# Padding small matmuls, cutting the prompt's value products to 32-column tiles with the sample's runs behind them, and pacing the sample's work over two stages

## The chip, the cores and the metric

The kernel runs on one core of one Trainium2 chip. The metric is the device time of one execution in microseconds (us). Before the change it is 3110.48 us, the median of three runs from 3101.09 to 3113.35.

The core's engines each run a list of instructions of their own, in the order that was laid out for it: TensorE (PE in the profile, with its weight loads as PEld), VectorE (DVE), ScalarE (ACT), GpSimd (POOL) and SyncE (SP). SP issues nearly all DMAs here.

## The reference, cut to what matters

One inference step of a decoder: one recurrent layer (RG-LRU), then one attention layer with forget gates that reads keys and values made once from the residual stream. It is done for a prompt of 2048 new tokens and for a sample of 8 sequences with 8 new tokens each, whose 4096 past tokens lie in pages of a cache.

```python
def fox_block(q, k, v, cq, ck, q_pos, k_pos):
    s = jnp.einsum('bqhd,bkhd->bhqk', q, k).astype(jnp.float32) * (HEAD_DIM ** -0.5)
    s = s + jnp.swapaxes(cq, 1, 2)[:, :, :, None] - jnp.swapaxes(ck, 1, 2)[:, :, None, :]
    mask = k_pos[None, :] <= q_pos[:, None]
    s = jnp.where(mask[None, None], s, -jnp.inf)
    p = jax.nn.softmax(s, axis=-1)
    return jnp.einsum('bhqk,bkhd->bqhd', p.astype(v.dtype), v)
```

There are 16 heads of 64 values. All data is float32. The keys and values of the past are 8 x 4096 rows of 16 x 64, read through `page_table`.

## The kernel before, in words

The program is written in an order that a builder then lays out on the engines: it keeps dependencies, and places ready instructions by priority (their place in the program) on a simulated time line. `tc.high_priority()` raises the priority, `tc.issue_after(i)` keeps instructions of an engine behind `i` on it. What the engines see is one fixed order each.

**Stages.** The recurrent layer over the prompt's halves, with the projections of the first half, comes first. The sample's decoding is cut into 16 turns (a sequence and half of the heads, `turns` at L1709); two are done early. Then `shared` (L1678) projects the prompt's second half to keys, values, queries and gates (`phase_b`), six steps alone and from about 1260 to 1703 us with the sample's work beside it; from 1703 to 2905 us `attention` (L1301) runs the prompt's attention, and `project` (L1589) makes the output rows until the end. The other 14 turns are the side work of the two middle stages.

**Side work.** `Side.along` (L1010) lets the main generator take a step, adds the cost that it yields, and takes as many steps of the side generator as bring its own cost to `share` times that (L1780). The side generator `beside` (L1774) is `decode` (L1024) and then `project_ready` (L1575), which loads and splits the output weights. The costs are written by hand: a turn yields `TURN` (L1019), 22,615.

**A turn of `decode`.** `keys` loads a quarter of a MB a page, four pages at a time (`pages`, L1053, on SP's queue into one of four `raw` buffers), transposes them on DVE (L1149), and after four such loads `scores` (L1113) does 64 matmuls of 128 x 32 with 128 moving columns in four column tiles. `new_scores` (L1127) does 32 small ones on 32 rows for the sample's own keys. `softmax` (L1157) finds the maxima (two small transposes, L1170 and L1175), exponentials and sums, and sends the probabilities through DRAM to another layout. `values` (L1217) loads the value pages and does 16 matmuls of 128 x 32 with 256 moving columns per four pages (`products`, L1225), at the end those of the new rows (L1235) and the sums over column tiles (L1257). One matmul of full float32 operands appears in the profile as two. `period` (L1265) interleaves the values of one turn with the keys of the next. A turn loads 64 pages: 32 of keys and 32 of values, for 8 of the 16 heads.

**The prompt's attention.** A unit (L1346) is a head and a block of 512 queries; the order of blocks turns round from head to head. For each of up to 16 blocks of 128 keys, two matmuls make the scores (`st`, L1527 and L1528, two PSUM buffers), on the diagonal a third adds the mask (L1530), ACT takes the exponential (L1536), and POOL sums the probabilities into `acc` (L1553; five buffers). After every fourth key block `product` (L1538), two steps later, multiplies the four blocks' probabilities by the values: the even blocks to one half of the PSUM tile's rows, the odd ones to the other, so that two tiles of 64 columns run side by side (L1547). `together` (L108) keeps such a group of matmuls in one piece. In between, `top` (L1384) computes the scores of later units in another layout for their maxima (`sx`, L1394, reduced on DVE), and `tops` (L1403) turns the maxima into rows by a transpose of 4 columns (L1411). `finish` (L1419) moves a unit's result out of PSUM; `total` (L1445) sums the four `acc` of a head by matmuls of 32 columns (L1450); `norm` (L1461) spreads the reciprocals by a matmul on 16 rows, or 4 in the last head (L1474), and multiplies by the gate. `later` (L339) is a list of calls by due step.

## Time and profile before

| | |
|---|---|
| median of three runs | 3110.48 us (3101.09 to 3113.35) |
| the profiled execution | 3106.18 us, its span 3104.4 us |
| TensorE's mean granted clock over the span | 0.958 |
| HBM read, written | 513.82 MB, 135.16 MB |
| sample's last value product ends | about 2580 us of the span |
| the prompt's last unit ends | about 2905 us |

A profile page gives busy time by engine, the chain of work that ended last (followed back from the end to what released each step) and the costliest groups of instructions. A group's line names the source line, engine, operation, the tile written and those read, the tile of the array in rows*columns, the moving operand and its count; then busy us, mean ns of one, and idle time of the engine just before with what ended it. A time line gives start and length in us, and the instructions merged in a row (`x16`). The ends of matmuls are modelled, so the starts are what to read there.

### The profile page before, as it was taken

Reading aid. Unit: us, or ns where it says so; the run is one execution under the profiler, and the core shown is the slowest. Engines: PE = TensorE matmul, PEld = TensorE weight load, DVE = VectorE, ACT = ScalarE, POOL = GpSimd, SP = SyncE. Lnnn points to the kernel's source line nnn. Section 1 sums busy time; section 2 is a strip of 40 time slices with the busy share of each in tenths; the row PEclk is TensorE's granted clock in tenths of the full one; section 3 lists DMA queues with packets and bytes.
Section 4 is the critical chain, followed back from the end, with each engine's and each line's share of the span. In section 5 each row is a group of like instructions: output and inputs, shape, how many; then the busy total and the mean of one; then the engine's idle time right before and its main releaser. Section 6 shows DMA issues by size and latency. Waiting matters only on the chain.

```text
span 3104.4 us, 58085 instructions
## 1 busy us (share of the span) xinstructions
PE 2856.4 (92%) x20446; PEld 2185.3 (70%) x20446; DVE 1805.1 (58%) x4014; ACT 1293.3 (42%) x2874; POOL 1155.4 (37%) x1251
## 2 busy tenths in 40 slices
PE   6998998998999989998998889898899989999798
PEld 5997888988999978886886555554555544544587
DVE  7876555424367756755755766666677655543244
ACT  4665432232346655333332344343444445455221
POOL 1653201000026531000002456565565757688322
PEclk9999999999999999998999899898999999999899
DMA  3225447788622266999999989999999985331343
GB/s 120 90 76 151 150 136 213 242 269 255 199 78 87 87 189 215 327 319 314 329 337 294 287 271 285 303 279 297 283 325 304 312 254 181 91 86 40 96 131 113
DMA packets 492854, 653.23 MB, mean 210 GB/s; under 512 B 91100, under 2 KB 292829, under 8 KB 485286
## 3 DMA queue, kind: packets, MB, share of 16 engines
q1 hardware_dynamic: 488934, 643.87, 66.2%
q10 hardware_dynamic: 3340, 3.56, 0.4%
q8 instruction: 161, 2.64, 0.3%
q0 software_dynamic: 288, 2.10, 0.2%
q14 instruction: 131, 1.07, 0.1%
HBM read 513.82 MB, written 135.16 MB: 209 GB/s over the span
## 4 chain that ended last, share of the span: by engine, by line
PE 45%; DMA 20%; DVE 7%; SPq 5%; ACT 4%; issue 3%; POOL 1%; ACTq 0%; DVEq 0%; POOLq 0%
PE ops L1547 6%; DMA raw<-in_cache_k_dram 4%; PE st L1527 4%; DMA raw<-in_cache_v_dram 4%; PE sx L1394 3%; PE y L368 3%; PE y L369 3%; PE y L370 3%; PE st L1528 3%; PE dO L1229 3%; PE dS L1119 3%; SPq L1066 2%; PE kv L368 2%; PE kv L369 2%; PE kv L370 2%
## 5 line engine op out<-in xcount | busy, mean ns | idle before, releaser
L106 POOL TENSOR_TENSOR acc<-acc,p 128x512 f32<-128x512 f32 (+3 forms) x576 | 638.6, 1109 | 315.9 <-PE ops L1547 263.8
L1536 ACT ACTIVATE p<-st 128x512 f32<-128x512 f32 (+3 forms) x576 | 288.5, 525 | 399.1 <-PE st L1528 203.0
L1149 DVE STREAM_TRANSPOSE ktr<-raw 128x1024 f32<-128x1024 f32 x256 | 305.6, 1223 | 147.9 <-DMA raw<-in_cache_k_dram 133.4
L1396 DVE TENSOR_REDUCE mxs<-sx 128x1 f32<-128x512 f32 x384 | 254.5, 681 | 165.7 <-PE sx L1394 164.5
L368 PE MATMUL kv<-wh,xh 128*128 128x256 f32 (+3 forms) x1088 | 311.8, 291 | 6.4 <-ACT wh L412 6.2
L369 PE MATMUL kv<-wl,xh 128*128 128x256 f32 (+3 forms) x1088 | 308.9, 287 | 4.4 <-DVE wl L413 4.2
L370 PE MATMUL kv<-wh,xl 128*128 128x256 f32 (+3 forms) x1088 | 309.4, 287 | 0.0
L1547 PE MATMUL ops<-p,vvt 128*64 128x512 f32 (+3 forms) x1152 | 294.6, 552 | 3.2 <-ACT p L1536 3.1
L1527 PE MATMUL st<-qa,ka 128*128 128x512 f32 (+3 forms) x640 | 277.1, 433 | 19.4 <-ACT p L1536 17.0
L1394 PE MATMUL sx<-kbt,qbt 96*128 96x512 f32 (+3 forms) x640 | 238.4, 433 | 31.2 <-DMA qbt<-qd 13.9
L1527 PEld LDWEIGHTS st<-qa,ka 128*128 128x128 f32 x640 | 125.7, 196 | 175.1 <-issue 114.5
L1528 PE MATMUL st<-qbt,kbt 128*128 128x512 f32 (+3 forms) x640 | 241.1, 378 | 0.0
L412 ACT ACTIVATE wh<-wst,gv 128x256 fp32r<-128x256 f32 (+1 forms) x384 | 164.3, 499 | 174.1 <-DMA wst<-in_b_w_in_dram 66.2
L413 DVE SCALAR_TENSOR_TENSOR wl<-wst,gv,wh 128x256 fp32r<-128x256 f32 (+1 forms) x384 | 170.6, 494 | 111.1 <-ACT wh L412 106.9
L368 PE MATMUL qg<-xh,wh 128*128 128x384 f32 (+2 forms) x640 | 228.2, 357 | 1.0 <-ACT wh L412 1.0
L370 PE MATMUL qg<-xh,wl 128*128 128x384 f32 (+2 forms) x640 | 226.9, 355 | 2.3 <-DVE wl L413 2.3
L369 PE MATMUL qg<-xl,wh 128*128 128x512 f32 (+2 forms) x640 | 227.3, 357 | 0.0
L1084 POOL TENSOR_TENSOR qw<-qb,amask 128x128 f32<-128x128 f32 x64 | 28.7, 455 | 504.6 <-PE dS L1119 358.6
L368 PEld LDWEIGHTS kv<-wh,xh 128*128 128x128 f32 (+1 forms) x1088 | 204.1, 189 | 14.5 <-ACT wh L412 7.1
L369 PEld LDWEIGHTS kv<-wl,xh 128*128 128x128 f32 (+1 forms) x1088 | 204.0, 189 | 7.7 <-DVE wl L413 5.7
L370 PEld LDWEIGHTS kv<-wh,xl 128*128 128x128 f32 (+1 forms) x1088 | 205.2, 189 | 2.9 <-issue 2.5
L1394 PEld LDWEIGHTS sx<-kbt,qbt 96*128 96x128 f32 x640 | 120.0, 204 | 102.9 <-issue 36.4
(283 smaller groups left out, 6482.2 us busy)
## 6 DMA issues: line engine op xcount, KB each, us to landing
raw<-in_cache_k_dram SPq DMA_DIRECT2D x512, 256.0 KB
raw<-in_cache_v_dram SPq DMA_DIRECT2D x512, 256.0 KB
wst<-in_w_kv_dram SPq DMA_DIRECT2D x48, 512.0 KB
wst<-in_b_w_in_dram SPq DMA_DIRECT2D x48, 512.0 KB
xt<-in_x_prompt_dram SPq DMA_DIRECT2D x32, 512.0 KB
wst<-in_a_w_in_dram SPq DMA_DIRECT2D x64, 256.0 KB
x<-x SPq DMA_DIRECT2D x32, 512.0 KB
out_dram<-kf SPq DMA_DIRECT2D x128, 128.0 KB
```

What stands on the lines that cost most here:

```text
L106: eng.tensor_tensor(out, a, b, op=op)
L368: T.matmul(ps, lh(k), rh(k), start=(k == 0), stop=False)
L369: T.matmul(ps, lh(k), rl(k), start=False, stop=False)
L370: T.matmul(ps, ll(k), rh(k), start=False, stop=(k == nk - 1))
L413: V.scalar_tensor_tensor(wl[:, k, :], st[:, k, :], gk, f(wh[:, k, :]), op0=ALU.mult, op1=ALU.subtract)
L1149: V.transpose(t.kts[pp][:, n], raw[:, :, pp * 256:(pp + 1) * 256])
L1394: T.matmul(ps[:, :w], qb[0:96, j * P:(j + 1) * P], kb[0:96, ck * 512:ck * 512 + w], start=True, stop=True)
L1396: V.reduce_max(mx[:, j, ck:ck + 1], ps[:, :w], axis=AX.X)
L1527: T.matmul(ps[:, lo:], ka[:, ks], qa[:, lo:], start=True, stop=False)
L1528: T.matmul(ps[:, lo:], kb[:, ks], qb[:, lo:], start=False, stop=(k < qc * 4))
L1536: pair.append((k, lo, p, A.activation(p[:, lo:], ps[:, lo:], AF.Exp)))
L1547: return T.matmul(ops[r:r + HD, lo:], vvs[h % 2][:, k, :], p[:, lo:], start=(k < 2), stop=(last and k >= todo[-1][0] - 1))
```

## The change

Five things are changed. The matmuls on few rows or columns (maxima of the sample, new keys and values, the prompt's row maxima, the gate's reciprocals) get operands of all 128 rows, and the transposed ones of 128 columns, with zeros around the data in tiles that are zeroed once. The prompt's value products are cut into column tiles of 32, four side by side. While attention runs, the sample's score and value runs and the heads' totals are no longer put in place at their point of the program but kept in a list (`Aside`), and those that were listed before the present step are emitted after each value product with their first matmul held behind that product's last one and at high priority; a need of their result empties the list earlier. The sums over a turn's column tiles become one of these calls. The share becomes the side work's whole cost (with 16,000 for `project_ready`) over 0.96 of the two stages' costs, 331,563 and 615,942 by the formula, in place of 1.13 times the turns' cost over 331,563 + 950,000.

```diff
-SHARE = 1.13
+EVEN = 0.96
...
+    behind = [None]
...
-        first = mms[0]().ins
+        with ExitStack() as es:
+            if behind[0]:
+                es.enter_context(tc.high_priority())
+                es.enter_context(tc.issue_after(behind[0]))
+            first = mms[0]().ins
...
             tc.add_manual_dep(first, d.ins.name, SYNC)
+        ins = first
...
             for mm in mms[1:]:
-                mm()
+                ins = mm().ins
+        return ins
+    class Aside:
+        def __init__(self):
+            self.live, self.q = False, []
+        def __call__(self, fn, key=None):
+            if self.live:
+                self.q.append((later.t, key, fn))
+            else:
+                fn()
+        def flush(self, ins=None, t=None):
+            while self.q and (t is None or self.q[0][0] < t):
+                behind[0] = ins
+                got = self.q.pop(0)[2]()
+                ins = ins and got
+            behind[0] = None
+        def waits(self, key):
+            return any(k == key for _, k, _ in self.q)
+        def need(self, key):
+            if self.waits(key):
+                self.flush()
+    aside = Aside()
...
-        rawn = pool.tile([32, 512], F32, name="rawn")
+        rawn = pool.tile([P, 512], F32, name="rawn")
         G.memset(rawn[:, :], 0.0)
+        pcs = [pool.tile([P, 64], F32, name=f"dpc{i}") for i in range(2)]
+        for pc in pcs:
+            G.memset(pc[:, :], 0.0)
+        mx = pool.tile([P, P], F32, name="dmx")
+        G.memset(mx[:, :], 0.0)
+        mr = pool.tile([P, 16, DS], F32, name="dmr")
+        G.memset(mr[:, :, :], 0.0)
...
-                together([partial(score, h, x, a) for h in range(4) for x in range(2) for a in range(4)])
+                ins = together([partial(score, h, x, a) for h in range(4) for x in range(2) for a in range(4)])
...
+                return ins
...
             def new_scores(raw):
-                kx = (spare() if ahead else pool.tile([P, 512], F32, name="kx", tag="kx"))[:32, :512]
+                kx = (spare() if ahead else pool.tile([P, 512], F32, name="kx", tag="kx"))[:, :512]
...
                 sp = bank("dS")
-                for h in range(8):
-                    for x in range(2):
-                        blk = (h * 2 + x) * 32
-                        T.matmul(sp[:32, h * DS:(h + 1) * DS], qw[:32, h // 2, h % 2 * 2 + x, :], kx[:, blk:blk + DS],
-                                 start=(x == 0), stop=(x == 1))
+                def score(h, x):
+                    blk = (h * 2 + x) * 32
+                    return T.matmul(sp[:32, h * DS:(h + 1) * DS], qw[:, h // 2, h % 2 * 2 + x, :], kx[:, blk:blk + DS],
+                                    start=(x == 0), stop=(x == 1))
+                ins = together([partial(score, h, x) for h in range(8) for x in range(2)])
...
+                return ins
...
                     fetch_c()
+                    aside.need("values")
...
                     if n == 3:
-                        dl.after(1 + pp, lambda g=g, pp=pp, kt=t.kts[pp]: scores(g, pp, kt))
+                        dl.after(1 + pp, lambda g=g, pp=pp, kt=t.kts[pp]: aside(lambda: scores(g, pp, kt), "scores"))
                     if (g, n, pp) == (1, 0, 0):
-                        new_scores(t.rown)
+                        aside(lambda: new_scores(t.rown), "scores")
...
                 yield HOP
-            mx = pool.tile([P, 8], F32, name="dmx", tag="dmx")
-            V.tensor_reduce(mx[:, :], gmx[:, :, :].rearrange("p g h -> p h g"), axis=AX.X, op=ALU.max)
+            for _ in range(6):
+                if aside.waits("scores"):
+                    yield HOP
+            aside.need("scores")
+            V.tensor_reduce(mx[:, :8], gmx[:, :, :].rearrange("p g h -> p h g"), axis=AX.X, op=ALU.max)
             mp = bank("dm")
-            T.transpose(mp[:8, :P], mx[:, :], ident[:, :])
+            T.transpose(mp[:, :P], mx[:, :], ident[:, :])
...
-            mr = pool.tile([8, 16, DS], F32, name="dmr", tag="dmr")
-            V.tensor_scalar(mr[:, :, :], m1[:, :].unsqueeze(1).to_broadcast([8, 16, DS]), -1.0, 0.0, op0=ALU.mult, op1=ALU.add)
-            T.transpose(mp[:, P:P + 8], mr[:, :, :].rearrange("h a q -> h (a q)"), ident[:8, :8])
+            V.tensor_scalar(mr[:8, :, :], m1[:, :].unsqueeze(1).to_broadcast([8, 16, DS]), -1.0, 0.0, op0=ALU.mult, op1=ALU.add)
+            T.matmul(mp[:, P:P + 8], mr[:, :, :].rearrange("h a q -> h (a q)"), ident[:, :8], start=True, stop=True)
...
-            pc = pool.tile([32, 64], F32, name="dpc", tag="dpc")
-            A.copy(pc[:, :].rearrange("p (h q) -> p h q", h=8), pt[:, :, :DS])
-            t.sx, t.pc = sx, pc
+            pc = t.pc = pcs[(b * 2 + hg) % 2]
+            A.copy(pc[:32, :].rearrange("p (h q) -> p h q", h=8), pt[:, :, :DS])
+            t.sx = sx
...
-                together([partial(mm, d, a) for d in range(4) for a in range(2)], came)
+                return together([partial(mm, d, a) for d in range(4) for a in range(2)], came)
...
             def new_products(raw):
-                for a in range(2):
-                    T.matmul(op[a * 32:(a + 1) * 32, :256], pc[:, a * 32:(a + 1) * 32], raw[:, a * 256:(a + 1) * 256],
-                             start=False, stop=True)
+                def mm(a):
+                    return T.matmul(op[a * 32:(a + 1) * 32, :256], pc[:, a * 32:(a + 1) * 32], raw[:, a * 256:(a + 1) * 256],
+                                    start=False, stop=True)
+                return together([partial(mm, a) for a in range(2)])
...
                 raw, came = t.raws.pop(0) if t.raws else pages(cache_v, b, hg, x)
-                dl.after(1, lambda i=x * 4, raw=raw, came=came: products(i, raw, came))
+                dl.after(1, lambda i=x * 4, raw=raw, came=came: aside(lambda: products(i, raw, came), "values"))
                 if x == 5:
+                    aside.need("scores")
...
                 return
-            dl.after(1, lambda: new_products(t.rown))
             dl.flush()
-            ob = pool.tile([P, 256], F32, name="ob", tag="ob")
-            A.copy(ob[:, :], op[:, :256])
+            def over_sums():
+                ins = new_products(t.rown)
+                ob = pool.tile([P, 256], F32, name="ob", tag="ob")
+                A.copy(ob[:, :], op[:, :256])
...
+                return ins
+            aside(over_sums, "values")
             yield PV
...
-        sel = pool.tile([16, 4, P], F32R, name="sel16")
-        sel4 = pool.tile([4, P], F32R, name="sel4")
+        sel = pool.tile([P, 4, P], F32R, name="sel16")
+        rr = pool.tile([P, 512], F32R, name="r16")
+        mrows = [pool.tile([P, P], F32, name=f"mrow{i}") for i in range(2)]
+        for t in (f(sel[:, :, :]), f(rr[:, :]), mrows[0][:, :], mrows[1][:, :]):
+            G.memset(t, 0.0)
         for h2 in range(2):
...
-            m = small.tile([P, 4], F32, name="mrow", tag="mrow")
-            V.tensor_reduce(m[:, :], mxs.pop(u)[:, :, :qc + 1], axis=AX.X, op=ALU.max)
+            m = mrows[u % 2]
+            V.tensor_reduce(m[:, :4], mxs.pop(u)[:, :, :qc + 1], axis=AX.X, op=ALU.max)
...
-                T.transpose(ps[:4, :P], m[:, :], ident[:, :])
+                T.transpose(ps[:, :P], m[:, :], ident[:, :])
...
             if len(accs) == 4 or h == H - 1:
-                later.after(2, lambda todo=accs[:]: total(h2, sums, todo, h >= H - 2))
+                whole = lambda todo=accs[:]: total(h2, sums, todo, h >= H - 2)
+                later.after(2, whole if h == H - 1 else lambda: aside(whole))
...
-            for qc, acc in todo:
-                T.matmul(ps[qc * 32:(qc + 1) * 32, :], ones[:, :32], acc[:, :], start=True, stop=True)
+            def mm(qc, acc):
+                return T.matmul(ps[qc * 32:(qc + 1) * 32, :], ones[:, :32], acc[:, :], start=True, stop=True)
+            ins = together([partial(mm, *x) for x in todo])
+            qc = todo[-1][0]
...
+            return ins
...
             for x in range(2):
-                S.dma_start(f(rr[x * w:(x + 1) * w, :]).rearrange("j (r c) -> j r c", r=16), f(rs[x][ps_, :]))
+                to = rr[x * 8:(x + 1) * 8, :] if n == 4 else rr[x * 8 + q0:x * 8 + q0 + 5:4, :]
+                S.dma_start(f(to).rearrange("j (r c) -> j r c", r=16), f(rs[x][ps_, :]))
...
-                T.matmul(ps[:, :], sel[:, qc, :] if n == 4 else sel4[:, :], rr[:w * 2, :], start=True, stop=True)
+                T.matmul(ps[:, :], sel[:, qc, :], rr[:, :], start=True, stop=True)
...
+        aside.live = True
...
-                    def mm(k, lo, p, _):
-                        r = k % 2 * HD
-                        return T.matmul(ops[r:r + HD, lo:], vvs[h % 2][:, k, :], p[:, lo:], start=(k < 2),
+                    def mm(k, lo, p, _, x):
+                        r, x = k % 2 * HD + x, slice(x, x + 32)
+                        return T.matmul(ops[r:r + 32, lo:], vvs[h % 2][:, k, x], p[:, lo:], start=(k < 2),
...
-                    together([partial(mm, *x) for x in todo], [todo[-1][3]])
+                    ins = together([partial(mm, *t, x) for t in todo for x in (0, 32)], [todo[-1][3]])
+                    aside.flush(ins, later.t)
...
         later.flush()
+        aside.flush()
+        aside.live = False
...
     side = Side(beside())
-    share = SHARE * (16 - FIRST) * TURN / (1024 / 128 * 24 * 4112 * 0.42 + 950000)
+    whole = 1024 / 128 * 24 * 4112 * 0.42
+    whole += H * sum((qc * 4 + 2.5) * 4.1 * 512 * 0.42 + (qc + 1) * 4 * 213 for qc in range(4))
+    share = ((16 - FIRST) * TURN + 16000) / (EVEN * whole)
...
```

25 lines of the change are left out of this document (11 added, 14 removed).

## The prediction

> **What bounds the kernel now.** I read the page's totals and its chain of waits first, then the busy times by stage, then what TensorE did and waited for in the attention stage, and last its order of time around a switch.
>
> ```profile
> span 3104.4 us, 58085 instructions
> PE 2856.4 (92%) x20446; PEld 2185.3 (70%) x20446; DVE 1805.1 (58%) x4014; ACT 1293.3 (42%) x2874; POOL 1155.4 (37%) x1251
> PE 45%; DMA 20%; DVE 7%; SPq 5%; ACT 4%; issue 3%; POOL 1%; ACTq 0%; DVEq 0%; POOLq 0%
> ```
> ```profile
> 1260.00:1703.00 443.00, 413.51 (x3900) 353.71 (x3898) 260.31 (x509) 151.59 (x393) 21.85 (x40) 0.96 0.99 323
> 1703.00:2585.00 882.00, 801.40 (x6794) 450.72 (x6794) 571.52 (x1181) 371.61 (x905) 521.15 (x502) 0.93 0.93 290
> 2585.00:2905.00 320.00, 293.70 (x1245) 152.01 (x1247) 144.35 (x330) 163.08 (x345) 244.32 (x213) 0.96 0.30 81
> 2905.00:3104.00 199.00, 177.85 (x730) 139.63 (x726) 77.81 (x245) 35.71 (x77) 43.69 (x36) 0.93 0.40 123
> ```
>
> The columns are the stretch, its length, busy us of PE, PEld, DVE, ACT, POOL, the granted clock, the DMA share and GB/s. The stretches are the second projection stage, attention with the sample beside it, attention alone, and the tail. TensorE is over 90% busy in the first three, so it is the bound, and time of it saved is time saved. But the projection stage has its DMA engines full as well (0.99), while the last 320 us of attention use 0.30 of them: the sample's work is spent too early. What TensorE loses is seen in the order of time:
>
> ```profile
> 2333.06 0.39 PE L1527 MATMUL st<-qa,ka 128*128 128x512 f32 x1
> 2333.29 0.39 PE L1528 MATMUL st<-qbt,kbt 128*128 128x512 f32 x1
> 2333.61 1.07 PE L1229 MATMUL dO<-raw,sx 128*32 128x256 f32 x16
> 2334.61 0.50 PE L1527 MATMUL st<-qa,ka 128*128 128x512 f32 x1
> 2334.95 0.39 PE L1528 MATMUL st<-qbt,kbt 128*128 128x512 f32 x1
> 2335.18 0.39 PE L1527 MATMUL st<-qa,ka 128*128 128x512 f32 x1
> ```
> ```profile
> 2008.74 1.07 PE L1229 MATMUL dO<-raw,sx 128*32 128x256 f32 x16
> 2009.63 0.40 PE L1119 MATMUL dS<-ktr,qw 128*32 128x128 f32 x8
> ```
>
> Start to start, full-array 512-column products follow each other in 0.23 us. Into a run of the sample it is 0.32 (+0.09), out of it the run lasts 1.00 where a second 32-column run follows after 0.89 (+0.11), and the first pair behind it takes 0.34 (+0.11). A run of the sample that stands alone thus costs 0.31 us beyond its arithmetic; one that joins another 32-column run costs nearly none of that.
>
> **The change, part by part.** *Runs behind the products.* The attention's own product run is there every four key blocks whether or not anything follows:
>
> ```profile
> 2530.80 0.64 PE L1547 MATMUL ops<-acc,vvt 128*64 128x512 f32 x1 [0.21 <-ACT acc L1536]
> 2531.28 0.59 PE L1547 MATMUL ops<-acc,vvt 128*64 128x512 f32 x1
> 2531.28 1.45 PE L1547 MATMUL ops<-p,vvt 128*64 128x512 f32 x5
> 2532.66 0.33 PE L1527 MATMUL st<-qa,ka 128*128 128x128 f32 x1
> ```
>
> Two 64-column tiles run side by side, a round in 0.48 and 0.46 on average afterwards: 1.86 us for four rounds. Cut into 32-column tiles, four run side by side and there are again four rounds of 512 columns, with twice the instructions; the sample's 16 matmuls in four rounds of 256 columns start four at a time and take 1.00 us, about half, so I take no change (bounds: 0.1 us either way on 160 runs, 16 us). What it buys is that the sample's runs need no switch:
>
> ```profile
> L1229 PE MATMUL dO<-raw,sx 128*32 128x256 f32 x1376 | 95.4, 400 | 20.8 <-DMA raw<-in_cache_v_dram 13.8 <-DMA sx<-pd 4.5 <-issue 2.5
> L1119 PE MATMUL dS<-ktr,qw 128*32 128x128 f32 x2432 | 80.9, 289 | 7.7 <-DVE ktr L1149 7.0 <-DVE mrow L1407 0.7
> L1450 PE MATMUL tot<-acc,ones 128*32 128x512 f32 x126 | 25.3, 603 | 1.0 <-DVE mxs L1396 1.0
> L1134 PE MATMUL dS<-sy,qw 32*32 32x8 f32 x288 | 14.2, 178 | 10.0 <-DVE sc L106 5.2 <-DVE mrow L1407 4.0 <-DVE sy L1129 0.9
> L1474 PE MATMUL rp<-r,sel 16*128 16x512 f32 (+1 forms) x30 | 13.1, 475 | 2.4 <-DMA r<-rs 2.4
> L1257 PE MATMUL dres<-sel,ob 128*128 128x16 f32 x88 | 11.6, 265 | 3.5 <-DVE mrow L1407 3.5
> L1175 PE MATMUL dm<-ident,dmr 8*128 8x8 f32 x10 | 2.3, 228 | 0.0
> ```
>
> These are TensorE's groups over attention's 1202 us (busy us, mean ns, then the idle time before them and what ended it). Runs: 1376/16 = 86 of values, 2432/64 = 38 of scores, 288/32 = 9 of new scores, 15 of totals; 30 gates and 10 maxima on few rows become full-array ones by padding. That is 188 round trips at 0.31 us = 58 us; a few of them already touch, so **-56** (bounds -28, if every second run isn't ready behind its product and goes alone, and -60).
>
> *Padding* adds no rounds. The row maxima's weight loads grow from 4 to 128 columns:
>
> ```profile
> L1411 PEld LDWEIGHTS mps<-ident,mrow 128*4 128x4 f32 x64 | 5.6, 87 | 14.7 <-DVE mrow L1407 8.7 <-issue 3.9 <-DVE gmx L1125 0.4
> L1528 PEld LDWEIGHTS st<-qbt,kbt 128*128 128x128 f32 x640 | 126.8, 198 | 10.3
> L1119 PEld LDWEIGHTS dS<-ktr,qw 128*32 128x32 f32 x2432 | 70.4, 117 | 18.1 <-issue 6.8 <-DVE ktr L1149 5.2 <-PE st L1528 1.4
> ```
>
> that is (198 - 87) ns x 74 = 8 us if nothing hid it; they load under the matmul before, so **0** (bounds 0 to +8). The new keys' 32-row matmuls become 128-row ones of 32 columns like the scores, whose matmuls pass at 80.9/2432 = 33 ns against 14.2/288 = 49 ns now: 0. The zeroing on POOL lies before its stages. The Trainium skill (TensorE: Matmul & The Clock Gate, "What overlaps and what doesn't") says weight loads overlap running matmuls only where row groups differ, which after padding is never so. By it each of the new scores' 32 loads of 117 ns would stand bare, 3.7 us a turn and some 20 us in all; the scores' rows above already use all rows and still pass in 33 ns, so the trace speaks against it here.
>
> *Pacing.* The share was 1.13 x 316,610 / 1,281,563 = 0.279 of the main work's cost and is 332,610 / (0.96 x 947,505) = 0.366: 1.31 times as much beside the projections, which obey it:
>
> ```profile
> DMA packets 102001, 142.93 MB, mean 323 GB/s; under 512 B 10226, under 2 KB 58098, under 8 KB 100771
> raw<-in_cache_k_dram SPq DMA_DIRECT2D x138, 256.0 KB
> raw<-in_cache_v_dram SPq DMA_DIRECT2D x105, 256.0 KB
> sc<-cd SPq DMA_DIRECT2D x5, 1024.0 KB
> pd<-sy SPq DMA_DIRECT2D x16, 256.0 KB
> sx<-pd SPq DMA_DIRECT2D x4, 1024.0 KB
> ```
> ```profile
> 1600.00:1650.00 50.00, 50.00 (x502) 44.49 (x501) 25.12 (x46) 17.74 (x43) 1.94 (x5) 1.00 1.00 345
> ```
>
> 243 page loads in 443 us are 3.8 of the 14 turns (a turn loads 64); 0.279 x 311,800 (the stage's cost behind its first six steps) / 22,615 (a turn's) gives 3.85. After, 5.0. A turn moves 64 x 0.262 MB, and 3.1 MB of probabilities and sums: 20 MB. So 1.2 turns add 24 MB where the engines are full, on the SP queue ahead of the stage's own weights and stores. At the mean 323 GB/s that is 74 us (upper end); if other traffic gives way, only the 1.2 turns' TensorE work of about 22 us each is added, 26 us (lower end: a turn is 8 x 0.89 + 4 x 64 x 0.033 us, some 2 us of small matmuls, and 14 switches). I take the best 50 us of the stage, 345 GB/s: 167 MB / 345 = 483 us, **+40**. Attention gets 9.0 turns in place of 10.2: 1.2 x 17.6 us, without switches, **-21**.
>
> *Waits.* The lines above hold 20.8 + 7.7 + 10.0 + 3.5 = 42 us in which TensorE waited for the sample's data in attention. There the pages now have until nine tenths of the stage, and the DMA engines are no longer full; but the runs' places are fixed. I take **-15** (bounds -42 and 0; a gain turned into a loss is a rival). The clock granted there is 0.93, beside 0.96 without the sample: up to 882 x 0.03 = 26 us; **-15**. The sample fills holes of the last 320 us, in whose list of waits stand (us, times, longest)
>
> ```profile
> PE st L1527 <- ACT p L1536: 9.3, 15, 2.6
> PE ops L1547 <- ACT p L1536: 4.4, 6, 1.5
> ```
>
> **-8** of 14. *New waits.* The totals go behind the next product, so at the seven even heads' second unit the first exponential waits for a free `acc` until that product and total are through, 1.86 us and about 1: +0 to +20, **+6**. The output weights come at the end of attention in place of 2585 us, and two early rows with them:
>
> ```profile
> L368 PE MATMUL y<-woh,ohT 128*64 128x512 f32 (+1 forms) x32 | 12.9, 402 | 0.8 <-ACT ohT L99 0.8
> ```
>
> three such lines (one for each product of the split operands), 38 us, that may fall into the tail; TensorE does them somewhere in any case: 0 to +38, **+8**.
>
> Sum: -56 + 40 - 21 - 15 - 15 - 8 + 6 + 8 = **-61 us**. The profiled execution took 3106.2 us (its span and 1.8 around it), so 3045; the three runs' median is 3110.5, 4 above it, so I say 3047.
>
> **The rivals.** *Runs stuck at a fixed place (slower).* TensorE runs its matmuls in the order laid out, and a value run put behind a product whose pages haven't landed holds all of attention: the scores behind it, and by them ACT's exponentials and POOL's sums. In the list of waits of the stretch with the sample:
>
> ```profile
> PE dO L1229 <- DMA raw<-in_cache_v_dram: 13.8, 11, 3.6
> ```
>
> (us in total, times, longest), so one is 1.25 us. At 72 value runs in attention each with one, +90, and neither the 15 us of waits nor those of the clock are won: -61 + 30 + 90 = +59, 3169. It decides from (61 - 30)/72 = 0.43 us a run. For it: pages are the queue's largest load, and their buffers are freed later, since a product may be up to four key blocks late. Against: attention's demand falls by a tenth and is spread over a longer stretch.
> *Another engine takes the saving (no change).* POOL is busy 244 of the last 320 us and the exponentials hold TensorE's two score buffers; a burst of product and sample leaves ACT idle first. Then half the switches are won: -28 + 40 - 21 + 6 + 8 = +5, 3115. Against: the waits for ACT are 14 us in 320.
> *It doesn't do what it says.* If runs aren't ready when the order is laid out, they fall between score products as now. For it: a run's first matmul is still placed when its operands are there by the builder's reckoning; against: it has raised priority as soon as they are. Then the padding alone, 40 x 0.31 = -12, with +40 - 21, 3117.
> *The clock is the larger half (faster).* 1202 us of attention at 0.94 on average, where the quoted 50 us had 1.00; at 0.99, 60 us in place of 15: 3002. The same page of the Trainium skill (Part 1, the HAM clock gate) has the clock at half rate after an idle window of about 3.4 us; by it, removing the long waits is what counts. The granted clock of the stretches agrees in direction, no row shows the threshold.
>
> **How the numbers follow.** Forecast 0.48, stuck runs 0.22, another engine 0.12, not as told 0.06, clock 0.12. No change is within 0.5% (15 us), about what this measurement can tell. Faster: 0.46 + 0.12 and a third of the two middle ones, 0.62; slower: 0.22, with a part of those and of the forecast's upper end, 0.30; same 0.08. The forecast's own range is 3005 to 3090; 8 in 10 reaches from below the clock's case, 2985, to the middle of the stuck runs', 3140.
>
> **What would show it.** Right: the sample's runs start within 0.1 us of the product's last round; gaps of 0.32 and 0.34 us beside them go; the projection stage lasts some 480 us; sample work lasts to nearly the end of attention; the clock is at 0.95 or more. Wrong: TensorE's idle before values and scores above 42 us, or a projection stage beyond 515 us.

## The result and the profile after

The changed kernel takes 3129.05 us, the median of 10 runs (3114.65 to 3139.16); the kernel before took 3108.08 us in runs on the same chips. The ratio is 1.0062, with a 95% interval of 1.0042 to 1.0081: slower, where 3047 us was forecast. The profiled execution took 3125.3 us, its span 3123.6, 19.2 above the span of before.

From the page of the changed kernel, the totals and the chain that ended last:

```profile
span 3123.6 us, 60831 instructions
PE 2825.2 (90%) x21742; PEld 2181.3 (70%) x21742; DVE 1812.0 (58%) x4012; ACT 1290.4 (41%) x2874; POOL 1156.7 (37%) x1263
PE 49%; DMA 20%; DVE 12%; ACT 7%; SPq 6%; issue 4%; POOL 2%; DVEq 0%; ACTq 0%; POOLq 0%
```

TensorE is busy 31 us less than before (2856.4), and yet the span is longer: what was saved came back as idle time, and more. On the chain DVE went from 7 to 12% and ACT from 4 to 7%. The stages of the changed kernel and then of the one before, cut at the first and the last score product of the prompt (columns as in the prediction: PE, PEld, DVE, ACT, POOL, clock, DMA share, GB/s):

```profile
1260.00:1755.00 495.00, 441.01 (x4162) 371.75 (x4160) 289.40 (x569) 158.45 (x422) 24.72 (x49) 0.93 0.98 320
1755.00:2766.00 1011.00, 901.58 (x8293) 510.15 (x8297) 625.31 (x1315) 449.96 (x1069) 650.80 (x614) 0.95 0.82 250
2766.00:2924.00 158.00, 136.39 (x767) 71.11 (x759) 68.00 (x133) 73.94 (x151) 114.14 (x96) 0.95 0.31 90
2924.00:3123.00 199.00, 176.58 (x744) 139.82 (x742) 79.22 (x247) 37.46 (x81) 43.67 (x36) 0.95 0.41 123
```
```profile
1260.00:1729.00 469.00, 426.43 (x3939) 360.48 (x3938) 273.14 (x543) 153.69 (x401) 21.85 (x40) 0.94 0.99 320
1729.00:2902.00 1173.00, 1080.71 (x7990) 595.00 (x7990) 701.20 (x1474) 530.69 (x1238) 765.47 (x714) 0.95 0.76 234
```

The projection stage grew by 26 us, attention shrank by 4 to 5 (1011 + 158 against 1173), the tail by 2. So the question is why attention gave so little. TensorE's groups there, after and before; the last numbers are the idle time before a group and what ended it:

```profile
L1618 PE MATMUL ops<-p,vvt 128*32 128x512 f32 (+2 forms) x2292 | 303.1, 566 | 10.9 <-ACT p L1606 10.4
L1597 PE MATMUL st<-qa,ka 128*128 128x512 f32 (+3 forms) x640 | 270.6, 423 | 25.7 <-ACT p L1606 21.3 <-ACT acc L1606 1.8 <-DMA qa<-qd 1.4
L1457 PE MATMUL sx<-kbt,qbt 96*128 96x512 f32 (+2 forms) x626 | 224.3, 416 | 46.4 <-DVE mxs L1459 31.5 <-DVE sgt L106 5.0 <-DVE nr_t L272 3.0
L1282 PE MATMUL dO<-raw,sx 128*32 128x256 f32 x1280 | 97.5, 400 | 13.4 <-DMA sx<-pd 7.6 <-DMA raw<-in_cache_v_dram 5.2 <-issue 0.6
L1618 PE MATMUL ops<-acc,vvt 128*32 128x512 f32 x252 | 74.9, 677 | 8.0 <-ACT p L1606 8.0
L1165 PE MATMUL dS<-ktr,qw 128*32 128x128 f32 x2304 | 74.5, 274 | 0.0
L1474 PE MATMUL mps<-ident,mrow 128*128 128x128 f32 x62 | 18.7, 302 | 16.0 <-DVE mrow L1470 16.0
L1181 PE MATMUL dS<-sy,qw 128*32 128x8 f32 x288 | 10.6, 177 | 4.1 <-DVE sc L106 3.6 <-DVE sy L1176 0.5
```
```profile
L1547 PE MATMUL ops<-p,vvt 128*64 128x512 f32 (+2 forms) x1146 | 293.1, 553 | 3.2 <-ACT p L1536 3.1
L1527 PE MATMUL st<-qa,ka 128*128 128x512 f32 (+1 forms) x639 | 276.8, 434 | 19.4 <-ACT p L1536 17.0 <-ACT acc L1536 1.7
L1394 PE MATMUL sx<-kbt,qbt 96*128 96x512 f32 (+2 forms) x620 | 228.0, 427 | 16.1 <-DVE mxs L1396 8.4 <-ACT qbt L1413 3.0 <-DVE mxs L1398 2.8
L1411 PE MATMUL mps<-ident,mrow 128*4 128x128 f32 x62 | 17.2, 278 | 4.1 <-DVE mrow L1407 4.0
```

Take the idle time in two heaps. Before the sample's matmuls (`dO`, `dS` and its small ones) it fell from 43.8 to 20.5 us, as forecast. Before the prompt's own (`st`, `sx`, `ops`, `mps`, `rp`, `tot`) it rose from 48.5 to 111.3. That heap is called the *own* waits below, the other the *sample's*. With the time lost to a clock below full (length times one minus the granted clock, by the clock's records) attention divides so:

| attention, us | length | idle: own | idle: sample's | lost to the clock | rest: work |
|---|---|---|---|---|---|
| before | 1173.3 | 48.5 | 43.8 | 63.3 | 1017.7 |
| after | 1168.3 | 111.3 | 20.5 | 62.8 | 973.7 |

The work did fall, by 44 us; 39 us came back as waits. Of the 63 us that the own waits grew by, 43 are waits for DVE (16 to 60 us) and 18 for the exponentials on ACT (22 to 40 us). One of them, from the order of time of the changed kernel, DVE first, then TensorE:

```profile
1933.65 0.14 DVE L1461 DVE_READ_ACCUMULATOR2_ANT mxs<- 128x1 f32 x1
1939.25 2.37 DVE L1200 STREAM_TRANSPOSE ktr<-raw 128x1024 f32<-128x1024 f32 x2 [5.46 <-DMA raw<-in_cache_k_dram]
1941.54 0.65 DVE L1459 TENSOR_REDUCE mxs<-sx 128x1 f32<-128x512 f32 x1
```
```profile
1934.48 1.70 PE L1282 MATMUL dO<-raw,sx 128*32 128x256 f32 x16
...
1938.40 0.73 PE L1457 MATMUL sx<-kbt,qbt 96*128 96x512 f32 x2
...
1942.25 0.51 PE L1457 MATMUL sx<-kbt,qbt 96*128 96x512 f32 x1 [2.87 <-DVE mxs L1459]
1942.59 0.60 PE L1597 MATMUL st<-qa,ka 128*128 128x512 f32 x1
```

DVE stands 5.46 us before a key transpose whose page is late, then transposes for 2.4 us. The prompt's maxima (`mxs`) are queued behind it, the three `sx` buffers fill, and TensorE stops for 2.87 us with its next score product (`st`) queued behind the waiting matmul. The Trainium skill (TensorE: Matmul & The Clock Gate, "What overlaps and what doesn't") states that matmuls start and end strictly in order; the trace agrees at 1942.25 and 1942.59. Of the ten stalls of over 2.2 us before `sx` and `mps` while the sample's work lasts, nine (30 us in all) have a key transpose on DVE that had waited 2.0 to 6.6 us. Why the page is late is in the waits over attention (DVE's list, then that of SP's queue), of the changed kernel and then of the one before:

```profile
DVE ktr L1200 <- DMA raw<-in_cache_k_dram: 109.4, 45, 6.6
...
SPq L1112 <- PE dO L1282: 43.3, 14, 9.1
```
```profile
DVE ktr L1149 <- DMA raw<-in_cache_k_dram: 59.9, 26, 5.1
...
SPq L1066 <- PE dO L1229: 2.5, 3, 2.0
```

The numbers are us in total, times and the longest. Page loads on SP's queue wait 43.3 us for value runs to give back a buffer, where they waited 2.5 us before; DVE's wait for key pages grew from 59.9 to 109.4 us. From the issue of the last of four value pages to their use 19.4 us pass (median, counted in the trace), where 8.9 passed before, with four buffers in all.

### The profile page after: what moved, and what is told of

Read it like the earlier page. It is cut to its first block, busy times and chain, and to the rows that moved or that the text cites. A ratio compares the mean times of both kernels' runs of the same rounds, so it can differ in the third digit from the quotient of the medians.

```text
span 3123.6 us, 60831 instructions
## 1 busy us (share of the span) xinstructions
PE 2825.2 (90%) x21742; PEld 2181.3 (70%) x21742; DVE 1812.0 (58%) x4012; ACT 1290.4 (41%) x2874; POOL 1156.7 (37%) x1263
## 4 chain that ended last, share of the span: by engine, by line
PE 49%; DMA 20%; DVE 12%; ACT 7%; SPq 6%; issue 4%; POOL 2%; DVEq 0%; ACTq 0%; POOLq 0%
PE ops L1618 6%; DMA raw<-in_cache_k_dram 6%; PE y L406 4%; PE y L407 4%; PE y L408 4%; PE st L1597 3%; PE sx L1457 3%; SPq L1112 3%; DMA raw<-in_cache_v_dram 3%; PE dO L1282 2%; PE st L1598 2%; DVE ktr L1200 2%; PE dS L1165 2%; PE kv L408 2%; DMA wst<-in_w_kv_dram 2%
## 5 line engine op out<-in xcount | busy, mean ns | idle before, releaser
L1618 PE MATMUL ops<-p,vvt 128*32 128x512 f32 (+3 forms) x2304 | 304.6, 565 | 10.9 <-ACT p L1606 10.4
L1597 PE MATMUL st<-qa,ka 128*128 128x512 f32 (+3 forms) x640 | 270.6, 423 | 25.7 <-ACT p L1606 21.3
L1457 PE MATMUL sx<-kbt,qbt 96*128 96x512 f32 (+3 forms) x640 | 231.3, 420 | 48.5 <-DVE mxs L1459 31.5
L451 DVE SCALAR_TENSOR_TENSOR wl<-wst,gv,wh 128x256 fp32r<-128x256 f32 (+1 forms) x384 | 169.6, 493 | 109.4 <-ACT wh L450 108.7
L406 PEld LDWEIGHTS kv<-wh,xh 128*128 128x128 f32 (+1 forms) x1088 | 205.7, 191 | 17.8 <-ACT wh L450 9.0
```

The costliest lines, as they stand in the source:

```text
L406: T.matmul(ps, lh(k), rh(k), start=(k == 0), stop=False)
L451: V.scalar_tensor_tensor(wl[:, k, :], st[:, k, :], gk, f(wh[:, k, :]), op0=ALU.mult, op1=ALU.subtract)
L1457: T.matmul(ps[:, :w], qb[0:96, j * P:(j + 1) * P], kb[0:96, ck * 512:ck * 512 + w], start=True, stop=True)
L1597: T.matmul(ps[:, lo:], ka[:, ks], qa[:, lo:], start=True, stop=False)
L1618: return T.matmul(ops[r:r + 32, lo:], vvs[h % 2][:, k, x], p[:, lo:], start=(k < 2), stop=(last and k >= todo[-1][0] - 1))
```

## The experiments

Each changes the kernel that the table names by what its diff shows. Where the lists are on and the order changes, `aside.need("values")` also stands ahead of the release of the sample's tiles. Times are medians, ratios those to the kernel before run on the same chip; waits and array changes are those of attention in the profiled execution. An array change is a matmul on another tiling of the array than the one before it; tiles of 32 columns, of 64 columns, of 32 rows or fewer and all others are told apart, and the transposes of 4 and 8 columns count with the others. "Lists" are the change's `Aside`. One execution is not the median: the profiled ones of runs 1, 2, 5, 9 and 12 lie 9 to 15 us above it, that of run 15 lies 10 us below.

| run | time, us | ratio, 95% | own waits | sample's | array changes |
|---|---|---|---|---|---|
| before | 3108.1 | 1 | 48.5 | 43.8 | 709 |
| after | 3129.1 | 1.0062 (1.0042-1.0081) | 111.3 | 20.5 | 418 |
| 1 transposes later | 3116.8 | 1.0022 (1.0004-1.0039) | 104.1 | 18.5 | 386 |
| 2 values free | 3115.8 | 1.0023 (1.0005-1.0042) | 76.8 | 50.7 | 519 |
| 3 lists off | 3089.7 | 0.9945 (0.992-0.997) | 56.2 | 41.6 | 592 |
| 4 old first pace | 3118.1 | 1.0033 (1.0012-1.0055) | 117.4 | 20.4 | 392 |
| 5 lists off, old pace | 3110.4 | 1.0010 (0.9991-1.0029) | 62.6 | 52.5 | 577 |
| 6 pace alone | 3133.1 | 1.0093 (1.0064-1.0121) | 52.0 | 38.2 | 659 |
| 7 listed, not held | 3099.7 | 0.9978 (0.9958-0.9999) | 59.0 | 41.4 | 590 |
| 8 totals listed | 3110.3 | 1.0014 (0.9995-1.0033) | 69.8 | 38.2 | 581 |
| 9 lists on, EVEN 0.94 | 3122.9 | 1.0039 (1.0013-1.0065) | 105.7 | 28.8 | 432 |
| 10 lists off, EVEN 0.94 | 3102.9 | 0.9988 (0.9962-1.0013) | 65.2 | 34.1 | 599 |
| 11 lists on, 3 buffers | 3176.4 | 1.0218 (1.0189-1.0247) | 131.9 | 25.8 | 410 |
| 12 lists off, 3 buffers | 3126.0 | 1.0052 (1.0029-1.0074) | 70.5 | 61.3 | 579 |
| 13 lists on, fixed keys | 3156.9 | 1.0176 (1.0153-1.02) | 113.2 | 13.7 | 382 |
| 14 lists off, fixed keys | 3151.8 | 1.0163 (1.0137-1.0188) | 63.1 | 39.9 | 577 |
| 15 lists off, 64 columns | 3106.9 | 1.0013 (0.9995-1.0032) | 68.1 | 30.0 | 596 |
| 16 lists off, EVEN 0.98 | 3100.0 | 0.9994 (0.9977-1.0012) | 56.5 | 41.7 | 601 |
| 17 held, not raised | 3138.6 | 1.0094 (1.0062-1.0126) | 123.1 | 24.8 | 436 |
| 18 scores free | 3151.1 | 1.0126 (1.0076-1.0176) | 132.1 | 28.1 | 460 |

The own waits fall apart into two groups. With value runs held behind the products (after, 1, 4, 9, 11, 13, 17, 18) they are 104 to 132 us; with no value run held (before, 2, 3, 5 to 8, 10, 12, 14 to 16) 49 to 77.

**Runs 1 to 4: which part of the change.** The theories: held page buffers make key pages late for DVE (H); bursts of product and run let the other engines run dry (B); the pace alone costs (P). Run 1 has the key transposes one load step later:

```diff
-                for pp in range(2):
-                    V.transpose(t.kts[pp][:, n], raw[:, :, pp * 256:(pp + 1) * 256])
+                t.hold.append((g, n, raw))
+                for pp in range(2):
+                    if len(t.hold) > ahead:
+                        turned(pp)
```


> The changed kernel (3129 us) with each group of key pages transposed on VectorE one step of the sample's work after its load in place of at once; the value runs stay behind the products. Theory H (held pages: value runs that wait for a product hold the page buffers, the next key pages come late, VectorE stands at their transposes with the prompt's maxima queued behind, and TensorE waits for those): VectorE's wait for key pages in attention falls from 110 us below 50, TensorE's idle time before sx and the row maxima from 65 us below 35, and the time by 25 to 35 us, to 3095 to 3105. Theory B (bursts: a product with the sample's runs in one piece lets ScalarE, GpSimd and VectorE run dry, and TensorE then waits for them): TensorE's idle time stays near 135 us and the time within 10 us of 3129. Theory P (the pace alone: the projection stage is 26 us longer, and attention simply gains less than thought): no change.

Run 2 takes the value runs out of the list:
```diff
-                dl.after(1, lambda i=x * 4, raw=raw, came=came: aside(lambda: products(i, raw, came), "values"))
+                dl.after(1, lambda i=x * 4, raw=raw, came=came: products(i, raw, came))
```


> The changed kernel (3129 us) with the value runs put in place at their point of the program again; scores, totals and a turn's last sums stay behind the products. H: the median from the last issue of a value group to its first product falls from 19 us to about 9, VectorE's wait for key pages from 110 to about 60 us and TensorE's idle time before sx and the row maxima from 65 to about 30 us; against it stand some 80 more lone runs at 0.31 us, 25 us; the time 3110 to 3125. B: TensorE's waits for ScalarE's exponentials (40 us) fall by half as the bursts are shorter, those for VectorE stay; 3125 to 3140. P: the switches alone, 3150.

Run 3 switches the lists off and leaves the rest of the change:
```diff
-        aside.live = True
+        aside.live = False
```


> The changed kernel (3129 us) with no run held back for a product: the 32-column products, the padding and the new pace stay. H: idle time in attention returns from 135 to about 97 us, changes of the array's tiling go from 418 to about 620, and the sample's work runs ahead again; with the longer projection stage 3120 to 3130. B: the same, so this run does not tell H from B. P: the projection stage keeps its 26 us and attention loses the 45 us of saved switches: 3150 to 3175.

Run 4 goes back to the old share beside the projections and raises it in attention:
```diff
-    side.along(gen, share)
+    side.along(gen, 0.2792)
...
-    side.along(attention(att), share)
+    side.along(attention(att), 0.4110)
```


> The changed kernel (3129 us) with the old share, 0.279, beside the projections, and 0.411 in place of 0.366 beside attention, so that the sample's work ends at the same place. P: the projection stage returns from 485 to about 445 us, attention grows by 20 us at most: 3105 to 3110. H: the projection stage returns too, but the denser work in attention meets the same held pages: VectorE's wait for key pages above 110 us, idle time above 145 us, and the time 3115 to 3135. B: as H by bursts that come more often, with the waits for the exponentials above 40 us.

Of these four, run 3 alone is clearly faster than both kernels, with the new pace: P alone isn't the cause. Run 1 halves DVE's idle time before the key transposes (119 to 59 us) and the own waits hardly move: H in its plain form isn't either. Run 2 brings the own waits down to 77 us, but 48.7 us of idle time then stand before its value runs, 33.1 of them for their pages. Run 4 wins back the projection stage (464 us against 495) and gives 19 us of it up in attention (1187.6).

**Runs 5, 6 and 8: the other parts alone.**
```diff
 # run 5: lists off, and both stages at the old share
+    share = 0.2792
     side.along(gen, share)
 # run 6: the kernel before with the new share
-    share = SHARE * (16 - FIRST) * TURN / (1024 / 128 * 24 * 4112 * 0.42 + 950000)
+    share = 0.3657
 # run 8: products, scores, new_scores and over_sums called at their place; total stays listed
-            aside(over_sums, "values")
+            over_sums()
```


> The changed kernel with the lists switched off and both stages' share back at the old 0.279; tiles of 32 columns and padding stay. If tiles and padding carry the gain of the run with the lists off (3090 us), it stays at 3085 to 3097 us and the projection stage goes back to some 465 us from the 484 it had there. If the new pace carries it, the time is that of the kernel before, 3103 to 3113 us. If both do, between them, about 3098 us.

> The kernel before with nothing changed but the share, 0.366 in place of 0.279. If the new pace carries the gain of the run with the lists off, 3088 to 3098 us. If it costs what the prediction said (+40 in the projection stage, -21 in attention), about 3127 us. If it is neutral and tiles and padding carry the gain, 3103 to 3113 us.

> The changed kernel with only the heads' totals listed and put behind a product; scores, values and column sums are free. If the sample's runs are what costs, 3085 to 3097 us, as with the lists off. If the totals behind the products cost (the first exponential of a unit waits for a free acc: 10.8 us of ACT's waits with the lists on), 3097 to 3110 us.

Run 6 by stage, to be laid beside the rows of before above:

```profile
1260.00:1775.00 515.00, 449.87 (x4320) 379.67 (x4318) 292.61 (x569) 155.76 (x411) 23.89 (x45) 0.91 0.98 318
1775.00:2543.00 768.00, 704.17 (x6040) 394.10 (x6043) 502.38 (x1042) 328.30 (x799) 453.34 (x436) 0.93 0.94 296
2543.00:2928.00 385.00, 358.63 (x1571) 186.28 (x1564) 177.83 (x404) 202.13 (x429) 310.55 (x274) 0.98 0.32 86
```

The projection stage grows by 46 us, attention shrinks by 20 (768 + 385 against 1173). Run 5 keeps the old pace: its array changes fall from 709 to 577, 66 round trips, and the work of attention from 1017.7 to 997.6 us, 0.30 us each. The time doesn't fall with it (ratio 1.0010): in its profiled execution idle rises from 92 to 115 us, the loss to the clock from 63 to 77. That execution is 15 us above the run's median, so these two show where time can go, not where the median's went. Run 8 is 20 us above run 3 but 7 and 10 above runs 10 and 16: no verdict on the totals.

**Runs 9, 10, 15 and 16: how much is the accident of one order.** A share 2% larger or smaller makes the builder lay out another order; run 15 has two tiles of 64 columns again.
```diff
 # runs 9 and 10; run 16: 0.98
-EVEN = 0.96
+EVEN = 0.94
 # run 15
-                        r, x = k % 2 * HD + x, slice(x, x + 32)
-                        return T.matmul(ops[r:r + 32, lo:], ...
+                        r, x = k % 2 * HD, slice(0, HD)
+                        return T.matmul(ops[r:r + HD, lo:], ...
-                    ins = together([partial(mm, *t, x) for t in todo for x in (0, 32)], [todo[-1][3]])
+                    ins = together([partial(mm, *t, x) for t in todo for x in (0,)], [todo[-1][3]])
```


> The changed kernel, lists on, with EVEN 0.94 in place of 0.96: the side work's share is 2% larger and everything else the same, so that the builder lays out another order. If the lists cost what the two first kernels show (3129 against 3090 us with them off), 3118 to 3135 us here, 25 us or more above the next run. If that difference is mostly an accident of one order, as the run with only the totals listed (20 us above the one without) hints, the two are within 12 us of each other.

> Lists off, EVEN 0.94. If 3090 us belongs to the form of the kernel, 3083 to 3098 us. If it was an accident of the order, 3100 to 3115 us.

> Lists off, the prompt's value products on two tiles of 64 columns again; padding and new share stay. If the tiles of 32 columns cost nothing and save switches only where a run of the sample stands beside a product, 3090 to 3105 us, within 10 us of the two runs with the lists off. If their twofold number of instructions costs TensorE, it is 10 us or more faster than those; if they are what lifted the free form over the kernel before, 3110 us or more.

> Lists off, EVEN 0.98: the side work's share 2% smaller. If the form with the lists off has a level of its own, 3085 to 3105 us and an idle of 50 to 70 us before the prompt's own matmuls. If it has none, it may land with the listed kernels, 3112 us or more.

With the lists off the three shares give 3089.7, 3102.9 and 3100.0 us, with them on two give 3129.1 and 3122.9. So orders of one form spread by some 13 us, and the forms lie 29 us apart (3126.0 against 3097.5, the means): the difference belongs to the form, while run 3's 0.9945 is the best of three, two of which can't be told from the kernel before. Run 15's work in attention (1003.3 us) is that of runs 3, 10 and 16 (1004.5, 997.9, 1003.6): cutting the products into 32 columns costs TensorE nothing.

**Runs 7 and 17: place, priority or lateness.** Run 7 keeps the lists and their late giving out, but drops the hold behind the product and the raised priority; run 17 drops the priority alone.
```diff
 # run 7
             while self.q and (t is None or self.q[0][0] < t):
-                behind[0] = ins
                 got = self.q.pop(0)[2]()
 # run 17
             if behind[0]:
-                es.enter_context(tc.high_priority())
                 es.enter_context(tc.issue_after(behind[0]))
```


> The changed kernel with the sample's runs still listed and given out after a value product, but without the order behind that product and without raised priority, so that the builder may place them among the score products. If the fixed place is what costs (theory of bursts), the time falls to 3085 to 3100 us, array changes rise to some 590 in attention and TensorE's idle falls to about 100 us from 132. If being given out late is what costs (a run, its buffers and the next loads all behind), the time stays at 3112 to 3130 us and the idle at 120 us or more, though the switches are lost.

> Lists on, the runs held behind the value product as in the change, but without raised priority: the builder may put score products between the product and the run. If the place straight behind the product is what costs (a run no longer fills a wait of the main work), part of the runs moves back among the score products, array changes in attention rise above 500, TensorE's idle before the prompt's own matmuls falls from 111 us to 60 to 85, and the time to 3095 to 3115 us. If it isn't the place but the order held on TensorE at all, idle stays above 95 us and the time at 3115 us or more.

TensorE's groups of run 7:

```profile
L1596 PE MATMUL st<-qa,ka 128*128 128x512 f32 (+3 forms) x640 | 275.1, 430 | 20.1 <-ACT p L1605 14.9 <-ACT acc L1605 2.5 <-DMA qa<-qd 1.7
L1456 PE MATMUL sx<-kbt,qbt 96*128 96x512 f32 (+2 forms) x626 | 232.4, 424 | 26.2 <-DVE mxs L1458 12.0 <-ACT qbt L1475 4.6 <-DVE mxs L1460 3.4
L1281 PE MATMUL dO<-raw,sx 128*32 128x256 f32 x1280 | 90.6, 403 | 33.3 <-DMA raw<-in_cache_v_dram 28.6 <-DMA sx<-pd 4.0 <-issue 0.6
L1473 PE MATMUL mps<-ident,mrow 128*128 128x128 f32 x62 | 18.5, 298 | 4.3 <-DVE mrow L1469 4.3
```

All of run 7's numbers came as the theory of the place had them. Against it the changed kernel's attention has 25 us less work (86 round trips fewer, 0.29 us each), 31 more idle and 9 more lost to the clock: +15 us, the rest is the projection stage. The own waits alone are 52 us above run 7's, twice what the round trips save. In the changed kernel 75 runs (heads' totals counted) follow a value product directly and 18 more follow another run there; in run 7 none follows a product. Run 17 leaves them there (75 and 11), with own waits of 123 us: the hold does it without the priority. As the runs didn't move, run 17 doesn't tell the place from the order, which it was meant to do.

**Run 18: which runs.** Only the score runs are taken out of the list.
```diff
-                        dl.after(1 + pp, lambda g=g, pp=pp, kt=t.kts[pp]: aside(lambda: scores(g, pp, kt), "scores"))
+                        dl.after(1 + pp, lambda g=g, pp=pp, kt=t.kts[pp]: scores(g, pp, kt))
...
-                        aside(lambda: new_scores(t.rown), "scores")
+                        new_scores(t.rown)
```


> Lists on for value runs, column sums and totals only; score runs go where the builder puts them. The counterpart of the run with the value runs free, which had 519 array changes, 77 us of idle before the prompt's own matmuls and 51 before the sample's. If that idle grows with the number of runs put straight behind a product (86 value runs here against 38 of scores there), 80 to 100 us here, and 3110 to 3125 us. If score runs alone do the harm, 50 to 65 us, and 3090 to 3105 us.

Its waits over attention (from the lists of the engines and of SP's queue), and then those of run 2, its counterpart:

```profile
DVE ktr L1200 <- DMA raw<-in_cache_k_dram: 151.3, 47, 11.3
PE mps L1474 <- DVE mrow L1470: 36.7, 12, 8.0
...
PE sx L1457 <- DVE mxs L1459: 21.5, 15, 4.8
...
SPq L1112 <- PE dO L1282: 33.3, 17, 7.1
SPq L1112 <- DVE ktr L1200: 30.2, 15, 5.9
```
```profile
DVE ktr L1200 <- DMA raw<-in_cache_k_dram: 70.8, 29, 5.4
...
PE sx L1457 <- DVE mxs L1459: 12.3, 11, 2.6
...
PE mps L1474 <- DVE mrow L1470: 7.2, 6, 2.3
...
SPq L1112 <- PE dO L1282: 4.7, 4, 2.1
```

Holding the value runs alone does all of the harm and more (own waits 132 us); holding the score runs alone does little of it (77). In run 18 27 us pass from the issue of a group of value pages to its use, in run 2 7.2, and the waits line up: SP's queue for value runs (33.3 against 4.7 us), DVE for key pages (151 against 71), TensorE for the maxima (58.2 against 19.5). Score runs that aren't held even made it worse, beyond what was expected; why wasn't tried further.

**Runs 11 to 14: is it the late key pages?** One buffer fewer, and key transposes that wait for no page.
```diff
 # runs 11 (lists on) and 12 (off)
-        yield from decode(dec, turns[FIRST:], 4, 2, True)
+        yield from decode(dec, turns[FIRST:], 3, 2, True)
 # runs 13 (lists on) and 14 (off)
-                    V.transpose(t.kts[pp][:, n], raw[:, :, pp * 256:(pp + 1) * 256])
+                    V.transpose(t.kts[pp][:, n].rearrange("p a (b c) -> p (a b) c", c=P),
+                                ident[:, :].unsqueeze(1).to_broadcast([P, 8, P]))
```


> The changed kernel, lists on, with three page buffers in place of four. If held page buffers are what costs (a value group is held 19 us behind its last issue with the lists on, 7 to 9 us without), the loss of one costs much here: 40 us or more over the changed kernel, 3170 us and above, and at least twice what the next run loses. If bursts on the engines are what costs, both lose about the same.

> Lists off, three page buffers. If held buffers are the cause with the lists on, little is lost here: at most 20 us, 3090 to 3112 us. If both kernels lose the same, the number of buffers sets the pace of the loads in either and the holding isn't what tells them apart.

> Lists on, but VectorE's key transposes read a fixed tile in place of the pages (the scores over the past are then not the reference's; the pages are loaded all the same, and their buffers come free on landing). If the lists cost because VectorE stands before key transposes whose pages are late (119 us in attention, 67 before) with the prompt's maxima queued behind it, TensorE's idle before the prompt's own matmuls falls from 111 us to 70 or less, and the time to 3075 to 3100 us, within 12 us of the next run. If the lists cost in another way (bursts, the order behind the products), that idle stays at 95 us or more and the time at least 20 us above the next run.

> Lists off, with the same fixed tile under the key transposes. If VectorE's wait for key pages is what tells the two forms apart, this gains little against the form with the lists off (3090 and 3103 us at two shares): 3075 to 3095 us.

A buffer is worth 47 us with the lists on and 36 with them off, not twice as much: the number of buffers sets the pace of the loads in both. (Against the means over the shares it is 50 and 28 us; with orders 13 us apart the ratio is known no better than that.) Run 12 has DVE idle 123 us before key transposes, as long as the changed kernel, and yet own waits of 70 only: that wait costs TensorE little by itself. That it costs where maxima that TensorE needs are queued behind it is a reading of the stalls above; run 12 doesn't show why its own waits stay low. Runs 13 and 14 leave the sample's past keys out of its scores, so their results aren't the reference's, and they tell only of time. Run 13's waits:

```profile
PE st L1597 <- ACT p L1606: 34.6, 54, 2.3
PE mps L1474 <- DVE mrow L1470: 17.6, 9, 6.2
PE rp L1543 <- DMA r<-rs: 15.5, 5, 8.5
PE sx L1457 <- DVE mxs L1459: 11.3, 14, 3.3
```

With the transposes' wait gone, the wait of `sx` for `mxs` falls from 31.5 to 11.3 us, and the two forms come within 5 us of each other, as theory H had it. That nearness is in part chance: attention is still 12 us longer with the lists on (27 us in the changed kernel against run 3), and run 14's longer projection stage makes up for it (529 us in run 13, 541 in run 14, from 495 and 484). The sum of the own waits stays at 113 us, as H's rival had it, 50 above run 14. The waits for the row maxima (`mps`, 16.0 to 17.6 us), which H should take away too, stayed; those for the gate's rows (`rp`, 2.7 to 15.5) and for the exponentials (`st` 21.3 to 34.6, `ops` 18.4 to 10.7) grew together by 18 us. Both runs take longer than the kernels that they change, which neither expectation saw: 39 and 51 more pages are loaded in the projection stage, so more of the side work runs there; that no late page holds it back any more would explain it and wasn't tested.

So late key pages are one path from a held value run to a waiting TensorE, shown link by link. Run 13's trace shows another of the same form, in which DVE stands for the totals' sums on their way through DRAM, with the row maxima behind it (DVE, then TensorE):

```profile
2250.50 0.35 DVE L1533 RECIPROCAL sums<-sums 128x32 f32<-128x32 f32 x1 [8.22 <-DMA sums<-cs]
2253.78 0.17 DVE L1470 TENSOR_REDUCE mrow<-mxs 128x4 f32<-128x16 f32 x1
```
```profile
2254.01 0.33 PE L1474 MATMUL mps<-ident,mrow 128*128 128x128 f32 x1 [4.85 <-DVE mrow L1470]
```

Two of its four stalls of over 2.2 us before `sx` and `mps` beside the sample's work (4.85 and 6.19 us) have such a wait of 8.22 or 7.28 us shortly before them, and a third (7.11 us) one of 9.77 us for POOL. DVE waits for the sums in the kernel before too (43.2 us), so what such a wait costs depends on what TensorE has to do meanwhile. How the whole loss divides among such paths is open. Bursts don't fit either: in the changed kernel, while the sample's work lasts, the stretches from one product to the next with two or more runs in them (36 of 138) hold 17.8 of 89 us of own waits, those with none (41) 41.9.

## Why the prediction was wrong

*What bounds the kernel.* TensorE, as read. That time saved on it is time saved was too short a step: in run 5 and in the changed kernel its work fell by 20 and 44 us and neither got faster. The own waits, 48.5 us in a stage of 1173, were small while runs of the sample, placed freely, stood among the score products (143 groups of value and score runs after the first to sixth score product behind a value product, none straight behind it). The trace of before could have told it: while the sample's work lasts (to 2580 us) the own waits are 24.5 us on 108 value products, 0.23 us each; in the 322 us without it 24.0 us on 51, 0.47 each. In the changed kernel they are 90.5 us on 138 while it lasts, 0.66 each. An estimate from these: had the held runs filled no wait at all, that would be 0.24 us on 138 products, 33 of the 59 us above the rate of before. The rest would be what the held runs delay.

*Switches, -56.* The price held: 0.31 us forecast, 0.30 in run 5, 0.29 against run 7, and 0.31 as the slope of a straight line through the work of all twenty kernels (less the sample's arithmetic, 0.89 us a value run and 2.1 a score run; the points scatter by 5 us). The number didn't: (709 - 418)/2 = 145 round trips went, not 188. Of the 44 us of work saved, 11 are 0.62 of a turn (at 17.6 us) that moved to the projection stage, so about 33 for the switches, inside the bounds of -28 and -60; that is 0.23 a round trip, and the kernel before lies 7 us under the line.

*Products of 32 columns 0, padding 0.* The first is right (run 15). No run has the padding alone; the two kernels without it, before and run 6, lie 7 and 2 us under the line just named, so it can have cost a few us.

*Pacing, +40 and -21.* Where it stood alone, run 6, the numbers came: +46 and -20. For the first it was luck in part: 24 MB more were forecast, at the stage's best rate of 345 GB/s; 14 MB came (0.8 turns for 1.2), and the rate stayed at the mean, 320 and 318 GB/s. The changed kernel had 0.62 turns more beside the projections, 8 to 9 MB, and paid 26 us, again what these take at 320 GB/s. Why the new pace costs 28 us on the kernel before and nothing with the lists off (runs 3, 10 and 16 are 7 to 21 us below run 5) is open.

*Waits, -15 with bounds of -42 and 0: the step that failed.* It counted the waits that stood before the sample's matmuls and asked how many would go. They went, 23 us of them. It didn't ask what TensorE would wait for once those runs no longer stood among the score products, and left a loss out of the bounds. The own waits rose by 63 us; sum +39, 54 off. That holding the value runs does it is shown by the groups of the table and by runs 2, 7 and 18; by which paths it does is shown for a part only.

*Clock, -15.* Measured 63.3 to 62.8 us, nothing. The term leaned on waits that would go, and as a whole they grew from 92 to 132 us. With the lists off, at the new pace and with four buffers, the loss was 38.5 to 55 us.

*Holes of the last 320 us, -8; accumulator, +6; late output weights, +8.* The sample's work reached to 2767 us instead of 2580, but the own waits of the last 320 us of attention grew all the same, from 24.0 to 32.6 us, and TensorE is busy 136 of the last 158 us, 86%, against 92% of the last 320 before. ACT waited 10.8 us for the totals before a unit's first exponential, 5.9 before; TensorE behind it 1.8, so +6 was too much. The tail took no more (199 us): nothing for the weights.

*The rivals.* "Runs stuck at a fixed place" had the right sign and a loss of the right order (+90 us of waits; the own waits rose by 63), but the wrong place: value runs waited less for their pages (13.8 to 5.2 us), not more. The clause that mattered stood in it as an aside, that buffers are freed later. "Another engine takes the saving" had the idea of the idle time and the wrong engines: DVE for most of it, ACT for the rest, not POOL.

*What would show it.* None of the signs named as proof of an error came: the idle time before values and scores was 17.5 us, not above 42, and the projection stage 495, not 515. Two of those for being right did come, the clock (0.95 beside the sample) and the stage's length (some 475 us by the prediction's cut, 443 before). All of them watched the side work or the clock. The sign to name was the idle time before the main work's matmuls. And 3129 us lies inside the range of 8 in 10 (2985 to 3140) only because that range reached into the stuck runs' case. The chances for "faster" add to 0.64, not to 0.62.

## What to carry to other kernels

Side work that is placed freely can fill the main work's waits. Before fixing it at one place, price both: what the fixed place saves (here 25 us against run 7) and what the main work will wait for more (here 52 us), and check how long the fixed work holds its input buffers, since the queue that refills them may feed another engine that the main work waits for. Before believing a gain of half a per cent from one version of a kernel whose order a program lays out, shake the order: here a 2% change of one number moved the time by 13 us.
